# The third block of 512 columns of gates, pool output and conv output computed with the weights standing, two more small moves in the layer norm's step list

## The chip, the cores and the metric

One core of a Trainium2 chip runs the whole kernel. The metric is the device time of one launch in microseconds (us); lower is better. The kernel before is timed in three runs and profiled in one more. "Engine" means one of PE (TensorE, matmuls), DVE (VectorE), ACT (ScalarE), POOL (GpSimd) and SP (SyncE, which issues most loads).

## The reference, cut to what matters

One layer of a decoder trunk on 256 tokens plus 16 prepended meta tokens, model width 2048, everything in float32:

```python
u = rms_norm(h, g_pre_mix[l])
proj = u @ w_in[l]
z_pool, v_conv, g_conv, gate_a, gate_b = jnp.split(proj, splits, axis=-1)   # 1024,1024,1024,2048,2048
y_a = causal_multiscale_pool(z_pool, w_pool_grp[l], pool_scale[l]) @ w_pool_out[l]   # 1024 -> 2048
y_b = conformer_conv(v_conv, g_conv, ...) @ w_conv_out[l]   # 31 taps, layer norm, silu; 1024 -> 2048
m = jax.nn.sigmoid(gate_a) * y_a + jax.nn.sigmoid(gate_b) * y_b
h = h + rms_norm(m @ w_o[l], g_post_mix[l])
u = rms_norm(h, g_pre_mlp[l])
f = jnp.square(jax.nn.relu(u @ w_up[l])) @ w_down[l]
h = h + rms_norm(f, g_post_mlp[l])
```

The change lies between `proj` and `m`; everything from `m @ w_o` on stays as it is.

## The kernel before, in words

**Three-product arithmetic.** Every float32 operand is split into a high part and a low part. ACT makes the high part (`hi`, a cast), DVE the low part (`lo`, a subtraction that needs `hi`). A product is then hi·hi + hi·lo + lo·hi, so each weight chunk of 1 MB costs one load, one ACT cast (L287), one DVE subtraction (L290) and its matmuls. `fetch` (L348) opens the next chunk: it issues the load and the two splits for the chunk two ahead of the one that PE is about to use, and empties the list `late`.

**Columns in blocks of 512.** The two gates, the pool's output projection and the conv's output projection each have 2048 output columns, worked in four blocks `n` = 0..3. `TURNED` says how many of the four are done one way; the rest go the other way.

- Weights standing ("turned", `project`, n < TURNED): a 128x128 piece of the weights is the stationary operand and the activations stream past, `mm2`: one matmul of 512 columns (L556: high weights, both halves of the activations) and one of 256 (L562: low weights). The result has features on partitions, in four accumulators `j` of 128 features; each has two halves that ACT copies (L934) and DVE adds (L937). For a gate, DVE then scales by the token's norm factor (L952) and ACT takes the sigmoid of a 128x1024 tile (L953).
- Activations standing (`project_t`, n >= TURNED): a 128-token piece of the activations stands and the weights stream, three matmuls of 512 columns per k (L901). The result has tokens on partitions, in two accumulators `t`. ACT takes the sigmoid straight from the accumulator with the token's factor (L944).

For the mixed `m`, features must lie on partitions. Turned blocks come out that way. The others are transposed on PE (L1038, four 128x128 transposes per token half), then split from the transposed accumulator (L1042 on ACT, L1045 on DVE). Blocks 0 and 1 are also copied into `A` (L1071), from which four sums for a Strassen-like product with `w_o` are formed.

The order of the blocks is n = 0, 1, 2, 3 for each gate (`gate00` to `gate03`, then `gate10` to `gate13`), then eight small products of the pool's groups (`acc_grp`, evacuated to `y` by ACT at L978 and DVE at L979), then the pool output `po` in the order POOLS (blocks that are not turned first, then the turned ones), then the conv output `co` 0 to 3, then the products with `w_o`.

**What sets the order of the side work.** Each engine works its instructions off in the order in which they were written. DVE and ACT have work beside the splits: the pooling, the 31 conv taps (L621) and the layer norm over the conv's channels (`ln_...`). This work is a list, `pending`, of items with a cost. `drain` is called after each piece of a block and lets items be written whose cost fits the credit: a turned block gives 2.0 us per chunk in four portions, the other kind 2.9 us in two (pool output: 1.5 and 2.4). Two markers stand in the list. `LATER` ends the current portion. `FETCH` holds the list until `late` has been emptied by the next `fetch`. `late` holds work that is written a little later so that its engine does not stand waiting, such as the sigmoid of a gate that waits for PE, or the square root of the norm:

```python
def ln_root():
    ...
    def root():
        nc.scalar.activation(ln["q"], ln["var"], AF.Sqrt)
        warm_up(AF.Sigmoid)
    late.append(root)
```

The square root needs another table on ACT than the sigmoid, so `root` costs a table load, the square root, a second table load and a one-column sigmoid (`warm`).

The layer norm's items in their order are: sum over channels (`add4`, `add2`, then `low`, then markers, then `across`, two matmuls on PE with a matrix of ones, key "m"), mean, centre in two halves, sum of squares in the same way (key "v"), `ln_root`, `ln_newton` (five small DVE instructions, L506 to L510), and for each half of the channels `normed` (L871), eight ACT instructions (L876, L877), `swish` (L882), and the split of the result into `s_act` (L885 on ACT, L888 on DVE), which the conv output reads.

**Banks.** `acc_tile` hands out six accumulator banks in turn. An accumulator can be written again only when its last reader has finished. The pool output's first two accumulators are the banks of the first two group products.

The functions that the diff touches:

Of the kernel before, what the change touches and what calls it, by code (L numbers as in the profile page):

```python
# [15 lines left out]
P = 128  # L16
# [102 lines left out]
def hybrid_block(ctx: ExitStack, tc: tile.TileContext, ins: dict, out: bass.AP):  # L119
    nc = tc.nc  # L120
# [5 lines left out]
    NT = T // P  # L126
# [28 lines left out]
    def f32(ap):  # L155
        return ap.bitcast(F32)
# [4 lines left out]
    def misc_tile(name):  # L161
        return psB.tile([P, CW], F32, tag="misc", name=name)
# [5 lines left out]
    pending = []  # L168
    late = []
    LATER = (0, None)  # L170
    FETCH = (0, late)
# [43 lines left out]
    for h in range(PW // HALF_CW):  # L215
        stream += columns(w_in, 0, KD, h * HALF_CW, HALF)
    standing_chunks = set()
    TURNED = 2

    def with_standing(chunks, n):  # L220
        if n < TURNED:
            standing_chunks.update(range(len(stream), len(stream) + len(chunks)))
        return chunks
# [3 lines left out]
    stream.append((w_grp.rearrange("g (k p) c -> p (g k) c", p=P), (NG * GD // P, GD)))  # L227
    POOLS = [*range(TURNED, NB), *range(TURNED)]
    for w, nk, ns in ((w_pool_out, KP, POOLS), (w_conv_out, KC, range(NB))):
# [305 lines left out]
    def sum_rows(dst, parts):  # L535

        for n, part in enumerate(parts):
            nc.tensor.matmul(dst, ones, part, start=n == 0, stop=n == len(parts) - 1)
# [269 lines left out]
    def sum_items(key, dst, src):  # L808

        def add4():  # L810
            nc.vector.tensor_add(dst()[:, 0:4, :], src()[:, 0:4, :], src()[:, 4:8, :])

        def add2():
            nc.vector.tensor_add(dst()[:, 0:2, :], dst()[:, 0:2, :], dst()[:, 2:4, :])
            nc.vector.tensor_add(dst()[:, 0, :], dst()[:, 0, :], dst()[:, 1, :])
            parts[:] = [tmp.tile([P, T], F32R, tag="v", bufs=5, name=f"cs_{p}_{key}")
                        for p in ("hi", "lo")]
            late.append(lambda: nc.scalar.copy(parts[0], dst()[:, 0, :]))

        def low():  # L820
            nc.vector.tensor_sub(parts[1], dst()[:, 0, :], f32(parts[0]))

        def across():
            ln[key] = ps = misc_tile(f"cs_{key}")
            sum_rows(ps[:, :T], parts)
        parts = []
        return [(1.1, add4), (1.0, add2), FETCH, (0.4, low)] + [LATER] * 3 + [(0, across)]

    def ln_start():
        ln["sq"] = big.tile([P, KC, T], F32, tag="a", name="sq")  # L830
# [59 lines left out]
        return [(1.1, f) for f in (normed, swish, low, high)]  # L890

    ln_halves = ln_items(0), ln_items(QW)
    for half, step in ((0, 0), (1, 0), (0, 1), (1, 1)):
        pending += [FETCH, ln_halves[half][step]]

    def block_t(acc, hi, lo, act, kc, nk, t, ks=range(CK)):
        ts_ = slice(t * P, (t + 1) * P)
# [44 lines left out]
    def evac_gate(b, n):  # L942
        def f(t, acc):
            late.append(lambda: nc.scalar.activation(gate_t(b, n, t), acc, AF.Sigmoid,  # L944
                                                     scale=sc["r"][:, t:t + 1]))
        return f

    def evac_gate_turned(b, n):
        dst = turned(sg[b][:, n])

        def scaled():
            nc.vector.tensor_mul(dst, dst, rb[:, None, M:].broadcast_to([P, CK, T]))  # L952
            late.append(lambda: nc.scalar.activation(dst, dst, AF.Sigmoid))  # L953

        def f(j, acc):
            two_parts(dst[:, j, :], acc, scaled if j == CK - 1 else None)
        return f

    for b in range(2):
        sg[b] = big.tile([P, NB, NT * CW], F32, tag=f"s{b}", name=f"sg{b}")  # L960
        for n in range(NB):
            if n < TURNED:
                project(u, KD, evac_gate_turned(b, n), f"gate{b}{n}", shape=(CK, CW), fill=2.0, mid=True)
            else:
                project_t(u_of, KD, evac_gate(b, n), f"gate{b}{n}", fill=2.9, mid=n == TURNED)

# [44 lines left out]
    for n in POOLS:  # L1011
        if n < TURNED:
            project(y, KP, evac_pool_turned(n), f"po{n}", shape=(CK, CW), fill=1.5, mid=True)
# [9 lines left out]
    for keys, op in ((((0, 0), (0, 1)), {}), (((0, 1), (1, 1)), {"accum_op": ALU.add})):  # L1023
# [4 lines left out]
    m = big.tile([P, LINE + KD * 2 * T], F32R, tag="um", name="m")[:, LINE:].rearrange(  # L1028
        "p (k a t) -> p k a t", k=KD, a=2)
# [29 lines left out]
    def evac_conv_turned(n):  # L1059
        mt = turned(mts[:, n % 2 * NT:(n % 2 + 1) * NT, :].rearrange("p a c -> p (a c)"))  # L1060
        dst = m[:, n * CK:(n + 1) * CK]

        def merged():
            nc.vector.tensor_mul(mt, mt, turned(sg[1][:, n]))
            nc.vector.tensor_add(mt, mt, turned(sg[0][:, n]))
            late.append(lambda: nc.scalar.copy(dst[:, :, 0, :], mt))

        def low():
            nc.vector.tensor_sub(dst[:, :, 1, :], mt, f32(dst[:, :, 0, :]))
            for t in range(NT):  # L1070
                nc.scalar.copy(A[:, t, n], mt[:, :, t * P:(t + 1) * P])  # L1071

        def f(j, acc):
            two_parts(mt[:, j, :], acc, merged if j == CK - 1 else None)
            if j == CK - 1:
                blocks.append(low)
        return f

    assert TURNED == 2

    def s_act_of(k):
        return ln["out"][:, k, :, :]
# [2 lines left out]
    A = big.tile([P, NT, 2, CK, P], F32, tag="a", name="A")  # L1085
# [122 lines left out]
    for i, s in enumerate(steps):  # L1208
        key = raw_key(s)
# [5 lines left out]
        if s == "P6":  # L1215
            key = block_key("P", "3")
# [284 lines left out]
    high, low = u2_tiles(0, 1, CK, CK)  # L1501
# [56 lines left out]
    for k0 in (3 * CK, 3 * CK + 2):  # L1558
        high, low = u2_tiles(0, NT, k0, 2)
# [700 lines left out]
```

## Time and profile before

| what | us |
|---|---|
| median of 3 runs | 1177.66 (1177.63 to 1177.91) |
| profiled execution, its own time | 1178.29 |
| its span, first to last instruction | 1176.3 |
| PE busy | 1166.8 (99%) |
| DVE busy | 1030.1 (88%) |
| ACT busy | 704.2 (60%) |
| granted TensorE clock, mean | 0.998 |

The profiled execution took 0.63 us more than the median; 1.99 us of its time lie outside the span. Matmuls are pipelined, so a matmul's shown duration (390 ns for 512 columns) is longer than the distance to the next one; durations of PE are therefore read from start to start.

### The profile page before, as it was taken

The numbers are of one execution on the slowest core, as the hardware profiler recorded it, in microseconds if no ns is written. First come the engines' busy times: TensorE is split into PE (matmuls) and PEld (weight loads), VectorE is DVE, ScalarE is ACT, GpSimd is POOL, SyncE is SP. The second block draws the span as 40 slices with busy tenths as digits, with TensorE's granted clock in tenths as the row PEclk, the third lists the DMA queues.
The fourth block names the chain that finished last, engine by engine and source line by source line (L and its number), as shares of the span: only waits on it lengthen the run. The fifth ranks groups of instructions, "written<-read, shape, count | busy, mean of one in ns | idle before, by whom it ended". The sixth has DMA issues, their size and how long they took to land.

```text
span 1176.3 us, 16264 instructions
## 1 busy us (share of the span) xinstructions
PE 1166.8 (99%) x6503; PEld 1021.4 (87%) x6503; DVE 1030.1 (88%) x1145; ACT 704.2 (60%) x754; POOL 121.0 (10%) x103
## 2 busy tenths in 40 slices
PE   9999999999999999999999999999999999999997
PEld 9999998888888888898888888888888888888886
DVE  6899987988577899988998899988898978999888
ACT  6543345444486666766767566666666666676673
POOL 1133222222000001000000000000000001000000
PEclk9999999999999999999999999999999999999999
DMA  8789989999856957849899988988998898899884
GB/s 296 245 263 274 288 264 275 320 280 273 279 173 239 296 215 217 286 161 337 242 312 300 223 287 220 289 275 217 271 287 217 248 313 206 266 264 252 298 233 182
DMA packets 185419, 305.43 MB, mean 260 GB/s; under 512 B 5153, under 2 KB 93281, under 8 KB 182528
## 3 DMA queue, kind: packets, MB, share of 16 engines
q1 hardware_dynamic: 157440, 239.62, 59.2%
q0 software_dynamic: 27296, 64.12, 27.2%
q8 instruction: 51, 0.84, 0.3%
q10 hardware_dynamic: 608, 0.66, 0.2%
q14 instruction: 24, 0.20, 0.0%
HBM read 300.18 MB, written 29.36 MB: 280 GB/s over the span
## 4 chain that ended last, share of the span: by engine, by line
PE 99%; DVE 1%; DVEq 0%; issue 0%; ACT 0%; ACTq 0%
PE bank_u L556 19%; PE bank_a L1964 11%; PE bank_u L562 9%; PE acc_gate L901 7%; PE bank_b L1964 7%; PE acc_up L1964 7%; PE o_c L1311 6%; PE acc_gate L556 5%; PE acc_z L551 4%; PE acc_v L551 3%; PE acc_g L551 3%; PE acc_gate L562 2%; PE acc_vg L551 2%; PE acc_co L901 2%; PE acc_po L901 2%; PE acc_up L556 1%
## 5 line engine op out<-in xcount | busy, mean ns | idle before, releaser
L556 PE MATMUL bank_u<-m,hi 128*128 128x512 f32 x960 | 329.8, 390 | 0.0
L562 PE MATMUL bank_u<-m,lo 128*128 128x256 f32 x960 | 266.0, 277 | 0.1
L287 ACT CAST hi<-raw 128x2048 fp32r<-128x2048 f32 (+2 forms) x94 | 150.9, 1618 | 161.1 <-issue 35.0
L290 DVE TENSOR_TENSOR lo<-raw,hi 128x2048 fp32r<-128x2048 f32 (+2 forms) x94 | 180.1, 1926 | 45.6 <-ACT hi L287 45.4
L556 PEld LDWEIGHTS bank_u<-m,hi 128*128 128x128 f32 x960 | 180.3, 188 | 37.7
L1748 DVE TENSOR_TENSOR lo<-raw_m,hi 128x2048 fp32r<-128x2048 f32 x75 | 171.4, 2287 | 23.1 <-ACT hi L1744 22.9
L1744 ACT CAST hi<-raw_m 128x2048 fp32r<-128x2048 f32 x75 | 143.2, 1911 | 68.2 <-PE bank_u L556 32.5
L562 PEld LDWEIGHTS bank_u<-m,lo 128*128 128x128 f32 x960 | 180.4, 188 | 2.2 <-DVE lo L1748 0.5
L621 DVE SCALAR_TENSOR_TENSOR c<-a,taps,c 128x256 f32<-128x256 f32 x240 | 99.2, 483 | 0.1
L1748 DVE TENSOR_TENSOR lo<-raw_a,hi 128x2048 fp32r<-128x2048 f32 x30 | 68.6, 2287 | 10.4 <-ACT hi L1744 10.3
L1744 ACT CAST hi<-raw_a 128x2048 fp32r<-128x2048 f32 x30 | 57.3, 1911 | 28.4 <-PE bank_u L556 8.0
L1964 PE MATMUL bank_a<-hi,forms 128*128 128x512 f32 (+1 forms) x232 | 74.1, 383 | 0.0
L345 POOL COPY rows_of<-rows_of 128x1 f32<-128x1 f32 x24 | 48.8, 2033 | 227.6 <-ACT rows_of L344 227.6
L556 PE MATMUL acc_gate<-u_um,hi 128*128 128x512 f32 x208 | 71.5, 390 | 0.0
L1748 DVE TENSOR_TENSOR lo<-raw_c,hi 128x2048 fp32r<-128x2048 f32 x26 | 59.5, 2289 | 10.3 <-ACT hi L1744 10.3
L1825 ACT COPY half<-bank_u 128x256 f32<-128x256 f32 x60 | 22.2, 370 | 73.3 <-PE bank_u L562 73.3
L901 PE MATMUL acc_gate<-hi,u_um 128*128 128x512 f32 x208 | 65.8, 390 | 0.0
L1744 ACT CAST hi<-raw_c 128x2048 fp32r<-128x2048 f32 x26 | 49.6, 1907 | 23.0 <-PE bank_u L556 14.5
L1964 PE MATMUL acc_up<-hi,forms 128*128 128x512 f32 x184 | 60.6, 390 | 0.0
L1964 PE MATMUL bank_b<-hi,forms 128*128 128x512 f32 (+1 forms) x184 | 58.3, 381 | 0.0
L562 PE MATMUL acc_gate<-u_um,lo 128*128 128x256 f32 x208 | 57.5, 276 | 0.0
L1766 POOL DMA_DIRECT2D raw_m<-in_w_down_dram x17 | 21.6, 1270 | 323.9 <-DVE fourth_pair L1748 153.9
(458 smaller groups left out, 2590.6 us busy)
## 6 DMA issues: line engine op xcount, KB each, us to landing
raw<-in_w_in_dram SPq DMA_DIRECT2D x52, 1024.0 KB, 7.0
raw_m<-in_w_down_dram SPq DMA_DIRECT2D x37, 1024.0 KB, 8.2
raw_m<-in_w_up_dram SPq DMA_DIRECT2D x33, 1024.0 KB, 7.3
sum_P<-in_w_down_dram POOLq DMA_DIRECT2D x18, 1024.0 KB, 9.1
raw_m<-in_w_down_dram POOLq DMA_DIRECT2D x17, 1024.0 KB, 9.4
raw_c<-in_w_up_dram SPq DMA_DIRECT2D x14, 1024.0 KB, 7.1
raw_a<-in_w_down_dram SPq DMA_DIRECT2D x13, 1024.0 KB, 6.9
raw_a<-in_w_up_dram SPq DMA_DIRECT2D x11, 1024.0 KB, 6.6
```

What stands on the lines that cost most here:

```text
L287: nc.scalar.copy(hi[:, sl, cs], raw[:, sl, cs])
L290: nc.vector.tensor_sub(lo[:, sl, cs], raw[:, sl, cs], f32(hi[:, sl, cs]))
L345: nc.gpsimd.tensor_copy(marks[:, RH * M // 2 + a:RH * M // 2 + a + 1], marks[:, a:a + 1])
L551: nc.tensor.matmul(acc, w[:, k[0], cs], act[:, k[1], a, off:], start=first and n == 0, stop=last and n == 2)
L556: nc.tensor.matmul(acc.rearrange("p (a t) -> p a t", a=2)[:, :, ts], hi[:, k[0], cs], act[:, k[1], :, off + ts.start:off + ts.stop], start ...
L562: nc.tensor.matmul(acc[:, :T], lo[:, k[0], cs], act[:, k[1], 0, off:], start=False, stop=stop, skip_group_check=True)
L621: nc.vector.scalar_tensor_tensor(c, conv["a"][:, q, i:i + T], taps[:, q, i:i + 1], c, op0=ALU.mult, op1=ALU.add)
L901: nc.tensor.matmul(acc, act(kk)[:, a_, ts_], w_[:, k, :], start=kk == 0 and n == 0, stop=kk == nk - 1 and n == 2)
L1311: nc.tensor.matmul(acc, form(k, a_), box[w_][:, k, :], start=start and k == 0 and n == 0, stop=stop and k == CK - 1 and n == 2, skip_group ...
L1744: nc.scalar.copy(box["hi"], raw)
L1748: nc.vector.tensor_sub(box["lo"], raw, f32(box["hi"]))
L1964: nc.tensor.matmul(acc, forms[h][:, f, k, a_, :], box[w_][:, k, cs], start=start and k == 0 and n == 0, stop=stop and k == KH - 1 and n == ...
```

## The change

`TURNED` goes from 2 to 3, so block 2 of both gates, of the pool output and of the conv output changes from the second way to the first. POOLS becomes 3, 0, 1, 2. Of the copies into `A` blocks 0 and 1 alone are kept. One `LATER` more stands before `across` of the first sum. In the norm's last steps one `FETCH` is taken out, so that `normed` of the second half and `swish` of the first may be written in one stretch.

```diff
-    TURNED = 2
+    TURNED = 3
...
-        return [(1.1, add4), (1.0, add2), FETCH, (0.4, low)] + [LATER] * 3 + [(0, across)]
+        return [(1.1, add4), (1.0, add2), FETCH, (0.4, low)] + [LATER] * (4 if key == "m" else 3) + [(0, across)]
...
-    for half, step in ((0, 0), (1, 0), (0, 1), (1, 1)):
-        pending += [FETCH, ln_halves[half][step]]
+    pending += [FETCH, ln_halves[0][0], FETCH, ln_halves[1][0], ln_halves[0][1],
+                FETCH, ln_halves[1][1]]
...
         def low():
             nc.vector.tensor_sub(dst[:, :, 1, :], mt, f32(dst[:, :, 0, :]))
-            for t in range(NT):
-                nc.scalar.copy(A[:, t, n], mt[:, :, t * P:(t + 1) * P])
+            if n < 2:
+                for t in range(NT):
+                    nc.scalar.copy(A[:, t, n], mt[:, :, t * P:(t + 1) * P])
...
-    assert TURNED == 2
+    assert TURNED == 3
```

Three places show how the instructions move. The numbers behind the names are buffer numbers; they differ between the two kernels and carry no meaning.

First, ACT at the end of the gates. `hi` is the high part of a chunk, `ln_q` the norm's square root, `sg1` the second gate, `acc_gate13_0` and `_1` the two accumulators of the last gate block, `y` the evacuated group products. Before:

```order
L287 CAST hi_57_3224<-raw_57_3223 128x2048
L855 ACT_TABLE_LOAD
L855 ACTIVATE ln_q_3221<-ln_var_3219 128x256
L375 ACT_TABLE_LOAD
L375 ACTIVATE warm_107<-ones_105 128x1
L944 ACTIVATE sg1_2583<-acc_gate13_0_3111,r_in_530 128x512
L944 ACTIVATE sg1_2583<-acc_gate13_1_3112,r_in_530 128x512
L287 CAST hi_58_3259<-raw_58_3258 128x2048
L978 ACTIVATE y_3255<-acc_grp_0_3264,vecs_110 128x256
```

ACT at the same place in the changed kernel:

```order
L287 CAST hi_57_3301<-raw_57_3300 128x2048
L944 ACTIVATE sg1_2616<-acc_gate13_0_3192,r_in_530 128x512
L944 ACTIVATE sg1_2616<-acc_gate13_1_3193,r_in_530 128x512
L855 ACT_TABLE_LOAD
L855 ACTIVATE ln_q_3335<-ln_var_3333 128x256
L375 ACT_TABLE_LOAD
L375 ACTIVATE warm_107<-ones_105 128x1
L287 CAST hi_58_3343<-raw_58_3342 128x2048
L978 ACTIVATE y_3337<-acc_grp_0_3348,vecs_110 128x256
```

The two table loads and the square root moved from ahead of the last gate's sigmoids to behind them. On PE the two matmuls of `across` for "v" moved with them, from inside the last gate block to behind its last matmul.

Second, DVE at the pool output, where the norm's last steps stand. `lo` is the low part of a chunk, `c` the conv's channels, `s_act` the norm's split result, `pairs` the room for a turned block's halves. Before:

```order
L290 TENSOR_TENSOR lo_61_3420<-raw_61_3418,hi_61_3419 128x2048
L882 TENSOR_TENSOR c_622<-c_622,sq_2934 128x1024 x2
L290 TENSOR_TENSOR lo_62_3461<-raw_62_3459,hi_62_3460 128x2048
L995 TENSOR_TENSOR sg0_1895<-acc_po3_0_3416,sg0_1895 128x512
L888 TENSOR_TENSOR s_act_3458<-c_622,s_act_3458 128x4x256
L995 TENSOR_TENSOR sg0_1895<-acc_po3_1_3417,sg0_1895 128x512
L888 TENSOR_TENSOR s_act_3458<-c_622,s_act_3458 128x4x256
L290 TENSOR_TENSOR lo_63_3501<-raw_63_3499,hi_63_3500 128x2048
L290 TENSOR_TENSOR lo_64_3539<-raw_64_3537,hi_64_3538 128x2048
L937 TENSOR_TENSOR pairs_3341<-pairs_3341,acc_po0_0_3495 128x256
```

DVE at the same place in the changed kernel:

```order
L882 TENSOR_TENSOR c_622<-c_622,sq_3054 128x1024
L290 TENSOR_TENSOR lo_61_3507<-raw_61_3505,hi_61_3506 128x2048
L882 TENSOR_TENSOR c_622<-c_622,sq_3054 128x1024
L290 TENSOR_TENSOR lo_62_3555<-raw_62_3553,hi_62_3554 128x2048
L937 TENSOR_TENSOR pairs_3425<-pairs_3425,acc_po0_0_3501 128x256
L1005 TENSOR_TENSOR sg0_1895<-pairs_3425,sg0_1895 128x256
L937 TENSOR_TENSOR pairs_3425<-pairs_3425,acc_po0_1_3502 128x256
```

Only one block that is not turned (block 3) now stands ahead of block 0, so block 0's first addition follows the split of chunk 62 where it followed that of chunk 64. The norm's last split (L888) moved behind block 0's additions.

Third, DVE from the conv output's third block to the products with `w_o`. `mts` holds the mixed block, `m` its split form, L1064 and L1065 multiply by the gate and add the pool's share. Before:

```order
L1054 TENSOR_TENSOR mts_3683<-acc_co2_0_3868,sg1_2583 128x512
L1055 TENSOR_TENSOR mts_3683<-mts_3683,sg0_1895 128x512
L1054 TENSOR_TENSOR mts_3683<-acc_co2_1_3869,sg1_2583 128x512
L1055 TENSOR_TENSOR mts_3683<-mts_3683,sg0_1895 128x512
L290 TENSOR_TENSOR lo_73_3950<-raw_73_3948,hi_73_3949 128x2048
L1045 TENSOR_TENSOR m_3681<-mt_2_0_3978,m_3681 128x4x128
L1045 TENSOR_TENSOR m_3681<-mt_2_1_3985,m_3681 128x4x128
L290 TENSOR_TENSOR lo_74_3994<-raw_74_3992,hi_74_3993 128x2048
L1054 TENSOR_TENSOR mts_3683<-acc_co3_0_3946,sg1_2583 128x512
```

DVE at the same place in the changed kernel:

```order
L937 TENSOR_TENSOR mts_3795<-mts_3795,acc_co2_0_3980 128x256
L937 TENSOR_TENSOR mts_3795<-mts_3795,acc_co2_1_3981 128x256
L937 TENSOR_TENSOR mts_3795<-mts_3795,acc_co2_2_3982 128x256
L937 TENSOR_TENSOR mts_3795<-mts_3795,acc_co2_3_3983 128x256
L1064 TENSOR_TENSOR mts_3795<-mts_3795,sg1_2616 128x1024
L1065 TENSOR_TENSOR mts_3795<-mts_3795,sg0_1895 128x1024
L290 TENSOR_TENSOR lo_73_4082<-raw_73_4080,hi_73_4081 128x2048
L1069 TENSOR_TENSOR m_3793<-mts_3795,m_3793 128x4x256
L290 TENSOR_TENSOR lo_74_4118<-raw_74_4116,hi_74_4117 128x2048
L1054 TENSOR_TENSOR mts_3795<-acc_co3_0_4078,sg1_2616 128x512
```

The block's own work on DVE is written as seven instructions where it was six, and the eight transposes on PE that stood between them are gone. From the products with `w_o` on, every engine's instructions stand in the same order in both kernels.

## The prediction

> **What bounds the kernel now.** I read the page's busy shares and the chain that ended last, then the starts of PE's stages in the timeline, then ACT and DVE around the places where the order changes.
>
> ```profile
> PE 1166.8 (99%) x6503; PEld 1021.4 (87%) x6503; DVE 1030.1 (88%) x1145; ACT 704.2 (60%) x754; POOL 121.0 (10%) x103
> PE 99%; DVE 1%; DVEq 0%; issue 0%; ACT 0%; ACTq 0%
> 153.10:421.60 268.50, 268.50 (x1407) 230.95 (x1406) 219.46 (x263) 142.84 (x157) 37.81 (x32) 1.00 0.85 262
> ```
>
> The chain is PE for 99%. The third row (columns: window, length, then busy time of PE, weight loads, DVE, ACT, POOL, then clock) covers all that the diff touches: PE never pauses, DVE has 49.0 us free, ACT 125.7. So only two things move the time: PE's own work, and any wait that a new order puts in front of PE. The starts of the stages give PE's work (columns: start, shown duration, engine, line):
>
> ```profile
> 153.13 0.40 PE L556 MATMUL acc_gate<-u_um,hi 128*128 128x512 f32 x1
> 196.66 0.40 PE L901 MATMUL acc_gate<-hi,u_um 128*128 128x512 f32 x1
> 240.20 0.40 PE L556 MATMUL acc_gate<-u_um,hi 128*128 128x512 f32 x1
> 333.56 0.40 PE L901 MATMUL acc_po<-hi,y 128*128 128x512 f32 x1
> 355.35 0.40 PE L556 MATMUL acc_po<-y,hi 128*128 128x512 f32 x1
> 377.12 0.39 PE L556 MATMUL acc_co<-s_act,hi 128*128 128x512 f32 x1
> 398.88 0.40 PE L901 MATMUL acc_co<-hi,s_act 128*128 128x512 f32 x1
> 421.59 0.39 PE L1311 MATMUL o_c<-hi,m 128*128 128x512 f32 x1
> 415.24 1.03 PE L1038 MATMUL mt<-ident,mts 128*128 128x128 f32 x8
> ```
>
> **Term 1, the blocks themselves: 0.** Two turned gate blocks take 196.66 - 153.13 = 43.53 us, two of the other kind 240.20 - 196.66 = 43.54. Pool output: 21.79 against 21.77. Both kinds stream as many columns. The page "TensorE: Matmul & The Clock Gate" of the Trainium skill (section "Wait — 56ns, not 53.3ns?") speaks against the change here: beside its columns each warm matmul costs some 2.5 ns, and the change makes 192 matmuls of 256 columns out of 96 of 512; an estimate by that rule is 96 x 2.5 ns = 0.24 us more. The two gate pairs, which differ by 64 matmuls, come out 0.01 us apart, so the trace does not agree, and I take 0.
>
> **Term 2, the transposes: -0.95.** Two turned conv blocks take 398.88 - 377.12 = 21.76 us, the two others 421.59 - 398.88 = 22.71. The excess is the eight transposes of block 2 (1.03 us with the last one's tail); block 3's are made later, inside the products with w_o, and stay. The change removes the eight.
>
> **Term 3, a new wait ahead of the pool output: +2.65.** Here ACT's order matters. Before:
>
> ```profile
> 322.35 1.91 ACT L287 CAST hi<-raw 128x2048 fp32r<-128x2048 f32 x1 [3.53 <-PE acc_gate L901]
> 324.28 1.28 ACT L855 ACT_TABLE_LOAD   x1
> 325.57 0.42 ACT L855 ACTIVATE ln_q<-ln_var 128x256 f32<-128x256 f32 x1
> 325.99 1.28 ACT L375 ACT_TABLE_LOAD   x1
> 327.29 0.20 ACT L375 ACTIVATE warm<-ones 128x1 f32<-128x1 f32 x1
> 327.40 1.30 ACT L944 ACTIVATE sg<-acc_gate,r_in 128x512 f32<-128x512 f32 x2
> 328.60 1.90 ACT L287 CAST hi<-raw 128x2048 fp32r<-128x2048 f32 x1
> 330.39 2.41 ACT L978 ACTIVATE y<-acc_grp,vecs 128x256 fp32r<-128x256 f32 x6
> ```
>
> The square root with its two table loads (324.28 to 327.40, 3.1 us) lies where ACT would otherwise wait for PE to finish the last gate block. DVE and PE behind it:
>
> ```profile
> 327.59 0.39 PE L901 MATMUL acc_gate<-hi,u_ux 128*128 128x512 f32 x1
> 322.11 0.28 PE L538 MATMUL cs_v<-cs_hi_v,ones 128*128 128x256 f32 x1
> 322.54 0.42 DVE L851 TENSOR_SCALAR ln_var<-cs_v 128x256 f32<-128x256 f32 x1 [1.40 <-PE cs_v L538]
> 330.53 2.29 DVE L290 TENSOR_TENSOR lo<-raw,hi 128x2048 fp32r<-128x2048 f32 x1 [3.94 <-ACT hi L287]
> 332.74 3.22 DVE L979 SCALAR_TENSOR_TENSOR y<-acc_grp,vecs,y 128x256 fp32r<-128x256 f32 x8
> ...
> L979 DVE SCALAR_TENSOR_TENSOR y<-acc_grp,vecs,y x8: 476/476/479, 332.7 to 335.5; 128x256 fp32r<-128x256 f32 x8
> ```
>
> The eight at 332.74 take 0.476 us each (last row: least, median and greatest, in ns) at a pitch of 0.39, so the first low part of y is ready at 333.22, and PE takes it up at 333.56, without a wait but with only 0.34 us to spare. PE's first matmul of the pool output needs exactly that instruction, because it also frees the first bank.
>
> In the changed kernel the norm's list runs one portion later: `across` for "v" comes behind the last gate matmul, and `root` behind both sigmoids. Step by step: the last gate matmul starts 0.23 earlier (the two matmuls of `across`, 0.11 apart, now follow it), at 327.36, and its shown end is 327.75. The second sigmoid, 0.65, runs to 328.43. The table load ends at 329.73 (ln_var, 0.4 us behind `across`, is there by 328.4), the square root at 330.15, the second load at 331.44, and the cast of chunk 58 starts 0.11 behind the warm instruction's start, at 331.56 instead of 328.60. Everything behind it on ACT and DVE moves by these 2.96 us: y's first low part ends at 333.22 + 2.96 = 336.18. PE arrives at 333.56 and waits 2.6 to 2.7 us, I take 2.65. Once it runs, it uses one y per 0.68 us and DVE makes one per 0.39, so no further wait follows there. Queued behind the late cast are the y parts (who wait on ACT) and `ln_newton`, normed and the split of chunk 59 on DVE; the last has some 2.5 us of cover. Bounds: not below 1.4 (if one table load of 1.28 overlapped something), not above 3.2 (if the sigmoid's start slipped by its own 0.65).
>
> **Term 4, a wait for a bank in the second turned pool block: +0.35.** From the rows before:
>
> ```profile
> 341.44 1.22 DVE L871 TENSOR_TENSOR c<-c,ln_r 128x1024 f32<-128x1024 f32 x1
> 342.70 0.60 ACT L876 ACTIVATE sq<-c,vecs 128x256 f32<-128x256 f32 x1 [1.54 <-DVE c L871]
> 347.22 1.89 ACT L287 CAST hi<-raw 128x2048 fp32r<-128x2048 f32 x1
> 353.54 1.89 ACT L287 CAST hi<-raw 128x2048 fp32r<-128x2048 f32 x1
> 355.46 2.29 DVE L290 TENSOR_TENSOR lo<-raw,hi 128x2048 fp32r<-128x2048 f32 x1 [0.57 <-ACT hi L287]
> 357.67 0.68 DVE L995 TENSOR_TENSOR sg<-acc_po,sg 128x512 f32<-128x512 f32 x1
> 365.54 0.41 DVE L937 TENSOR_TENSOR pairs<-pairs,acc_po 128x256 f32<-128x256 f32 x1
> ```
>
> The norm's eight ACT instructions per half take 347.22 - 342.70 = 4.52. After term 3 `normed` of the first half starts 2.9 us later (344.36), the eight end at 350.1, a cast (1.8), the second eight, and the cast of chunk 62 run from 356.4 to 358.3; its low part on DVE ends its slot at 360.6 (355.46 to 357.67: 2.21). Only then comes block 0's first addition, to 361.0. That addition frees the bank which PE wants for block 1's third accumulator, at 336.2 + 2 x 10.89 + 2.72 = 360.7. A wait of 0.35; bounds 0 and 0.8, since it is the end of a long chain. Before, additions like it (365.54) had cover because the norm was through.
>
> **What I cost at nothing.** DVE gets some 9 us more: per gate four additions of 0.41 and one scaling of 1.2, twice; in the pool output 2.0; in the conv output 1.3. They fall into its 49.0 free us. ACT's twelve extra copies and one larger sigmoid per gate fall into 125.7. The smaller portions write 9 us less of the pending list (0.9 x 4 chunks x 2 gates, 0.9 x 2 in the pool), so the norm's last split lands in block 1 of the pool output, about 10 us ahead of the conv output that reads it. The extra LATER makes PE reach `across` of "m" 6.8 us into its stretch; the operand needs a cast (1.9), a split (2.3) and its own 0.4 first, 4.7 in all, so 2.1 us are spare (0.8 without it). SP's loads keep number and order; POOL's are untouched. The one place without much cover is the start of the products with w_o:
>
> ```profile
> 398.90:422.00 23.10, 23.10 (x108) 19.21 (x107) 20.53 (x20) 11.30 (x11) 0.00 (x0) 1.00 0.67 214
> 432.14 0.68 DVE L1303 TENSOR_TENSOR forms_o<-A,forms_o 128x512 fp32r<-128x512 f32 x1
> 433.84 0.39 PE L1311 MATMUL o_c<-hi,forms_o 128*128 128x512 f32 x1
> ```
>
> DVE's form is ready at 432.82, PE wants it at 433.84: 1.0 to spare. DVE comes there later against PE by at most 1.3 (more work) + 0.95 (PE's transposes gone), less the 2.57 us that it idled in the stage. I take 0, bound 1.2.
>
> **Sum.** 0 - 0.95 + 2.65 + 0.35 = +2.05 us. On the profiled execution that is 1178.29 + 2.05 = 1180.34; the median before stands 0.63 lower, so the forecast for the median is 1177.66 + 2.05 = 1179.7, that is +0.17%. I count less than 0.2% (2.4 us: below 1175.3, above 1180.0) as no change that a measurement can tell.
>
> **Rivals.**
> - The wait of term 3 is hidden: something lets ACT run the loads early, or PE arrives late anyway. Then only the transposes count: 1177.66 - 0.95 = 1176.7. The instruction order speaks against it. Chance 0.12.
> - The pause slows the clock. At launch PE's matmuls of 128 columns come twice as slowly as later, though the granted clock is written as 1.00:
>
> ```profile
> 1.13 3.35 PE L452 MATMUL idle<-rb 128*128 128x128 f32 x14 [1.13 <-DVE rb L366]
> 5.96 1.28 PE L452 MATMUL idle<-rb 128*128 128x128 f32 x6
> ```
>
> 0.21 us each until about 6.9, against 0.11 for the transposes at 415.24: 5.8 us at half pace. If a pause of 2.65 us brings that back for as long, it costs half of 5.8, 2.9 us, and the time is 1182.6, slower. It decides once 0.3 us are lost so. No pause of that length is in the trace to judge by. The Trainium skill, same page, section "Part 1: The HAM clock gate (the "warmup" mystery)", puts the fall to half clock behind an idle window of about 3.4 us; by that rule a pause of 2.65 is too short. Chance 0.08.
> - DVE is late at the products with w_o, or term 3 or 4 at its upper bound: 0.3 to 1.2 more, 1180.1 to 1181. Chance 0.22, slower too.
>
> **How the numbers follow.** The forecast's own case, terms 3 and 4 near their values, 0.58: 1178.9 to 1180.0, no change. With the first rival, no change has 0.12 + 0.55, slower 0.08 + 0.22 + 0.01, and faster keeps 0.02, since nothing on PE's path could give 2.4 us. The range goes from the first rival's 1176.7 to 1181.0, leaving out the clock and some of either tail.
>
> **What would show it.** Right: on PE a gap of about 2.6 us ahead of the first L901 of `acc_po`, released by DVE's y (L979); ACT with the table loads behind the sigmoids; the three turned conv blocks at 32.6 us and no transposes at block 2; a small gap in the second turned pool block, released by L937. Wrong: PE without a gap there; 128-column pace doubled behind it; new gaps on L1311 behind forms_o or on gates behind L290.

## The result, and the profile after

| | us |
|---|---|
| before, median of 8 runs beside it | 1177.91 (1177.39 to 1178.36) |
| after, median of 8 runs | 1181.66 (1180.43 to 1184.25) |
| ratio of after to before | 1.0034, 95% interval 1.0024 to 1.0043 |
| profiled execution of after, its own time | 1182.13 (before 1178.29) |
| its span | 1180.3 (before 1176.3) |

The change costs 3.75 us by the medians and 3.84 us by the two profiled executions. The forecast was +2.05 us, with a range up to 1181.0: the result lies above it.

The page of after, its busy times, then the starts of PE's stages in the timeline (start, shown duration, engine, line):

```profile
PE 1167.9 (99%) x6591; PEld 1024.7 (87%) x6591; DVE 1037.3 (88%) x1162; ACT 708.6 (60%) x767; POOL 117.6 (10%) x103
153.30:425.60 272.30, 269.69 (x1494) 234.75 (x1493) 226.68 (x280) 147.02 (x170) 34.36 (x32) 1.00 0.85 259
153.32 0.39 PE L556 MATMUL acc_gate<-u_um,hi 128*128 128x512 f32 x1
333.69 0.28 PE L551 MATMUL acc_grp<-d,lo 128*128 128x256 f32 x1
336.51 0.50 PE L901 MATMUL acc_po<-hi,y 128*128 128x512 f32 x1 [2.54 <-DVE y L979]
381.08 0.39 PE L556 MATMUL acc_co<-s_act,hi 128*128 128x512 f32 x1
414.68 0.40 PE L901 MATMUL acc_co<-hi,s_act 128*128 128x512 f32 x1
425.62 0.39 PE L1312 MATMUL o_c<-hi,m 128*128 128x512 f32 x1
```

The busy shares say 99% for PE as before; only the window row shows that PE now pauses (269.69 busy of 272.30). By stage, from the starts here and those of before:

| stage | before | after | difference |
|---|---|---|---|
| start of the gates (nothing ahead of it was touched) | 153.13 | 153.32 | +0.19 |
| gates, up to the first group product (328.06 after, 327.81 before) | 174.68 | 174.74 | +0.06 |
| group products, up to the pool output | 5.75 | 8.45 | +2.70 |
| pool output | 43.56 | 44.57 | +1.01 |
| conv output | 44.47 | 44.54 | +0.07 |
| from the products with w_o to the end | 754.74 | 754.72 | -0.02 |

The 2.70 is one gap. ACT and DVE there in after, with the bracket's idle time and its releaser:

```profile
328.02 0.69 ACT L944 ACTIVATE sg<-acc_gate,r_in 128x512 f32<-128x512 f32 x1 [2.03 <-PE acc_gate L901]
328.73 1.28 ACT L855 ACT_TABLE_LOAD   x1
330.44 1.28 ACT L375 ACT_TABLE_LOAD   x1
331.85 1.89 ACT L287 CAST hi<-raw 128x2048 fp32r<-128x2048 f32 x1
335.98 3.22 DVE L979 SCALAR_TENSOR_TENSOR y<-acc_grp,vecs,y 128x256 fp32r<-128x256 f32 x8
```

ACT waits 2.03 us for the second sigmoid's accumulator and only then loads its tables, the cast comes at 331.85 instead of 328.60, DVE's y at 335.98 instead of 332.74, and PE takes y up at 336.51.

The pool output's 1.01 and the conv's 0.07 need the pace of single matmuls. PE and DVE around the second turned pool block, then PE near the end of the turned conv blocks:

```profile
360.12 0.39 PE L556 MATMUL acc_po<-y,hi 128*128 128x512 f32 x1
360.34 0.28 PE L562 MATMUL acc_po<-y,lo 128*128 128x256 f32 x1
360.46 0.39 PE L556 MATMUL acc_po<-y,hi 128*128 128x512 f32 x1
361.02 0.28 PE L562 MATMUL acc_po<-y,lo 128*128 128x256 f32 x1
361.37 0.50 PE L556 MATMUL acc_po<-y,hi 128*128 128x512 f32 x1
358.70 2.29 DVE L290 TENSOR_TENSOR lo<-raw,hi 128x2048 fp32r<-128x2048 f32 x1 [0.57 <-ACT hi L287]
360.90 0.41 DVE L937 TENSOR_TENSOR pairs<-pairs,acc_po 128x256 f32<-128x256 f32 x1
...
412.58 0.39 PE L556 MATMUL acc_co<-s_act,hi 128*128 128x512 f32 x1
412.93 0.40 PE L556 MATMUL acc_co<-s_act,hi 128*128 128x512 f32 x1
413.28 0.39 PE L556 MATMUL acc_co<-s_act,hi 128*128 128x512 f32 x1
```

Two things are to be seen. At 361.02 the next matmul comes 0.35 us later instead of 0.11: the wait of 0.24 for the bank that DVE's addition at 360.90 frees. The first matmul behind it takes 0.34 to the next start instead of 0.23 (361.37 to 361.71), as the one at 336.51 does (to 336.84). And behind that wait a pair of one 512- and one 256-column matmul takes 0.35 us (412.58, 412.93, 413.28), where ahead of it it took 0.34 (360.12 to 360.46). From 361.37 to 414.68, where the block of the other kind begins, lie 152 such pairs: (53.31 - 0.11 for the first matmul after the wait) / 152 = 350 ns a pair, against 340, so 152 x 0.010 = 1.5 us. The granted clock is 1.00 throughout. So the pool output's 1.01 is 0.11 (first matmul after the gap) + 0.24 + 0.11 (bank wait and the matmul after it) + 56 pairs x 0.010; the conv's 0.07 is 96 pairs x 0.010 = 0.96 less 0.89 for the transposes that are gone.

### The profile page after: what moved, and what is told of

It is laid out like the page before. It is cut to its first block, busy times and chain, and to the rows that moved or that the text cites. A ratio compares the mean times of both kernels' runs of the same rounds, so it can differ in the third digit from the quotient of the medians.

```text
span 1180.3 us, 16472 instructions
## 1 busy us (share of the span) xinstructions
PE 1167.9 (99%) x6591; PEld 1024.7 (87%) x6591; DVE 1037.3 (88%) x1162; ACT 708.6 (60%) x767; POOL 117.6 (10%) x103
## 4 chain that ended last, share of the span: by engine, by line
PE 96%; DVE 2%; ACT 1%; issue 0%; DVEq 0%; ACTq 0%
PE bank_u L556 18%; PE bank_a L1965 11%; PE bank_u L562 9%; PE acc_gate L556 7%; PE bank_b L1965 7%; PE acc_up L1965 7%; PE o_c L1312 6%; PE acc_z L551 4%; PE acc_gate L562 4%; PE acc_gate L901 4%; PE acc_v L551 3%; PE acc_g L551 3%; PE acc_vg L551 2%; PE acc_co L556 2%; PE acc_up L556 1%; PE acc_po L556 1%
## 5 line engine op out<-in xcount | busy, mean ns | idle before, releaser
L562 PE MATMUL bank_u<-m,lo 128*128 128x256 f32 x960 | 265.4, 276 | 0.3 <-DVE lo L1749 0.3
L562 PEld LDWEIGHTS bank_u<-m,lo 128*128 128x128 f32 x960 | 180.2, 188 | 2.4 <-DVE lo L1749 0.7
L556 PE MATMUL acc_gate<-u_um,hi 128*128 128x512 f32 x312 | 107.3, 389 | 0.0
L562 PE MATMUL acc_gate<-u_um,lo 128*128 128x256 f32 x312 | 86.1, 276 | 0.0
L556 PEld LDWEIGHTS acc_gate<-u_um,hi 128*128 128x128 f32 x312 | 58.6, 188 | 12.2
L345 POOL COPY rows_of<-rows_of 128x1 f32<-128x1 f32 x24 | 45.2, 1883 | 233.2 <-ACT rows_of L344 233.2
L562 PEld LDWEIGHTS acc_gate<-u_um,lo 128*128 128x128 f32 x312 | 58.6, 188 | 0.0
```

Source lines behind the costliest of these rows:

```text
L345: nc.gpsimd.tensor_copy(marks[:, RH * M // 2 + a:RH * M // 2 + a + 1], marks[:, a:a + 1])
L556: nc.tensor.matmul(acc.rearrange("p (a t) -> p a t", a=2)[:, :, ts], hi[:, k[0], cs], act[:, k[1], :, off + ts.start:off + ts.stop], start ...
L562: nc.tensor.matmul(acc[:, :T], lo[:, k[0], cs], act[:, k[1], 0, off:], start=False, stop=stop, skip_group_check=True)
```

## The experiments

Theory after the result: three separate losses, the extra `LATER` (ACT's table loads behind the last sigmoids, 2.7 us), the bank wait (0.35), and a slow pace of the turned blocks, 1.5 us, which something sets. Rivals: the third block itself costs the 2.7 us; the slow pace belongs to the third block, not to the wait. Medians below stand beside runs of before on the same chip, whose medians are 1177.59 (experiments 1 to 4), 1177.81 (5 and 7 to 9) and 1177.70 (6 and 11). What is read from a profile holds for the one execution that was profiled.

**1. The square root ahead of the sigmoids again**, by another way than the old order:

```diff
-    [LATER] * (4 if key == "m" else 3)
+    [LATER] * (4 if key == "m" else 2)
...
-        late.append(root)
+        late.insert(0, root)
```

> The changed kernel with the norm's square root and its two table loads written ahead of the last gate's two sigmoids (one LATER less before across of v, root put first in the list). Theory W (waits): the 2.8 us gap of PE ahead of the pool output comes from the table loads behind the sigmoids, so it is gone. Block 0's first addition then ends at about 358.1, where PE wants its bank at 358.1: no wait or under 0.1. If PE does not wait there, matmuls go 227/113 ns apart to the end of the conv output and the time is 1177.0 (before 1177.9 - 0.95 + 0.1); if the least wait is enough for the slow pace (232/117 ns), it is about 1178.5. Rival P (pace of position): three turned blocks after each other run at the slow pace by themselves; then 1178.5 with no wait at all.

Measured: 1179.61 (11 runs, 1177.53 to 1180.85), ratio 1.0015 (1.0006 to 1.0024). The expectation missed: the gap ahead of the pool output did not go but shrank from 2.70 to 1.03 us, and a bank wait of 0.24 and the slow pace (152 pairs) stayed. ACT in this kernel:

```profile
323.75 1.28 ACT L855 ACT_TABLE_LOAD   x1
326.43 0.42 ACT L855 ACTIVATE ln_q<-ln_var 128x256 f32<-128x256 f32 x1 [1.39 <-DVE ln_var L851]
326.85 1.28 ACT L375 ACT_TABLE_LOAD   x1
328.25 1.25 ACT L944 ACTIVATE sg<-acc_gate,r_in 128x512 f32<-128x512 f32 x2
```

The first load is covered, but the square root waits 1.39 us for DVE's `ln_var`. So the gap follows the place of the loads, and this way of moving them covers only part of it.

**2. Spare banks for the second turned pool block**, so that its last two accumulators wait for nobody:

```diff
-        accs = [acc[:, :width] for acc in acc_tiles(name, cw // P)]
+        tiles = acc_tiles(name, cw // P if name != "po1" else 2)
+        tiles += [misc_tile(f"acc_{name}_{j}") for j in range(len(tiles), cw // P)]
+        accs = [acc[:, :width] for acc in tiles]
```

> The changed kernel with two of the four accumulators of pool block 1 in the two spare banks, so that none has to wait for block 0's additions; ACT's order stays. Theory W: the 2.8 us gap stays, the 0.35 us wait at 361 is gone, and with it the slow pace behind it (53 us at +2.8%, 1.5 us): 1181.7 - 0.35 - 1.5 = 1179.9. Rival P: the wait is gone but matmuls still go 232/117 ns apart from there on: 1181.3.

Measured: 1181.59 (7 runs, 1180.06 to 1183.64), ratio 1.0028 (1.0017 to 1.0040). In the trace it went as the theory had it: no bank wait and no slow pace behind it, the turned blocks of pool and conv output at 32.65 and 32.64 us where after has 33.56 and 33.60, and the gap stayed. But the median is that of after, 1181.66, and not the 1179.9 expected, since something else stood in the profiled execution, which was the slowest of the seven (columns of the windows as above, clock before the DMA share):

```profile
336.05 0.79 PE L903 MATMUL acc_po<-hi,y 128*128 128x512 f32 x1 [2.54 <-DVE y L981]
330.00:336.00 6.00, 3.51 (x30) 3.31 (x28) 2.69 (x3) 5.99 (x11) 0.00 (x0) 0.95 0.14 55
336.00:342.00 6.00, 5.95 (x14) 4.69 (x15) 5.86 (x12) 2.00 (x2) 0.00 (x0) 0.50 0.52 178
342.00:348.00 6.00, 6.00 (x27) 4.90 (x27) 4.75 (x4) 3.21 (x4) 0.00 (x0) 0.98 0.39 130
```

Behind the same pause as in after, the granted clock was 0.50 for 6.83 us, and in 6.00 us PE ran 14 matmuls instead of some 27. Block 3 of the pool output took 13.89 us (336.05 to 349.95) where after needs 11.02, so 2.9 us were lost. After's own profile has the same pause and 1.00. So such a pause slows the clock in some executions and not in others. Each execution also lists its mean clock: here the two fastest, 1180.06 and 1180.18, have 0.998, the others, 1181.00 to 1183.64, have 0.996 and 0.997.

**3. The edits of experiments 1 and 2 together.**

> Both of these edits. Theory W: neither gap nor wait, pace 227/113 ns throughout but for the 4 us behind across of m in gate block 2: 1177.9 - 0.95 + 0.1 = 1177.0, 0.9 faster than before. Rival P: slow pace in the pool and conv blocks all the same: 1178.5.

Measured: 1178.26 (11 runs, 1177.45 to 1179.07), ratio 1.0005 (0.9997 to 1.0014). Against experiment 1 this is -1.35 us, for the bank wait and the slow pace (by the traces 0.35 + 1.5, less a new wait of 0.21 at the transposes of block 3, which is 1.6).

**4. The third block alone**: the extra `LATER` and the new chunks of the norm's last steps undone.

```diff
-    [LATER] * (4 if key == "m" else 3)
+    [LATER] * 3
...
-    pending += [FETCH, ln_halves[0][0], FETCH, ln_halves[1][0], ln_halves[0][1],
-                FETCH, ln_halves[1][1]]
+    for half, step in ((0, 0), (1, 0), (0, 1), (1, 1)):
+        pending += [FETCH, ln_halves[half][step]]
```

> The changed kernel with the other two parts undone: four chunks for the norm's last steps and three LATER before across of m, so that only the third turned block is left of the change. Theory W: ACT's order at the end of the gates is the same, gap and wait as well: 1181.7, within 0.4. Rival M (the small moves cost the time): 1178 or less.

Measured: 1179.38 (11 runs, 1177.84 to 1180.24), ratio 1.0012 (1.0004 to 1.0021). The expectation missed. There is no gap ahead of the pool output, but the bank wait is 1.2 us, with the slow pace behind it (152 pairs). ACT, PE and DVE in this kernel:

```profile
324.29 1.28 ACT L855 ACT_TABLE_LOAD   x1
327.41 1.31 ACT L944 ACTIVATE sg<-acc_gate,r_in 128x512 f32<-128x512 f32 x2
357.99 0.28 PE L562 MATMUL acc_po<-y,lo 128*128 128x256 f32 x1
359.30 0.50 PE L556 MATMUL acc_po<-y,hi 128*128 128x512 f32 x1 [1.03 <-DVE pairs L937]
357.69 1.22 DVE L882 TENSOR_TENSOR c<-c,sq 128x1024 f32<-128x1024 f32 x1
358.83 0.41 DVE L937 TENSOR_TENSOR pairs<-pairs,acc_po 128x256 f32<-128x256 f32 x1
```

The loads stand ahead of the sigmoids, as before the change. And the four chunks put `swish` (L882) straight ahead of the addition that PE waits for.

**5. The third block and the three chunks, without the extra `LATER`.**

```diff
-    [LATER] * (4 if key == "m" else 3)
+    [LATER] * 3
```

> The changed kernel without the extra LATER; three turned blocks and three chunks stay. Theory L (the LATER moved the norm's list one portion on and so the square root behind the sigmoids): no gap ahead of the pool output; a wait for block 0's addition of 0.1 to 1.2 us and the slow pace behind it stay: 1179.4. Rival C (the three chunks are what moved it): gap of 2.7 us, 1181.7.

Measured: 1178.40 (11 runs, 1177.11 to 1179.63), ratio 1.0006 (0.9997 to 1.0015). No gap; the bank wait is down to 0.05 us (PE L562 at 357.54, next at 357.70 instead of 357.65), and still the slow pace begins there (152 pairs). Each against its own runs of before, after stands at +3.75, this kernel at +0.59 and that of experiment 4 at +1.79. So the extra step of patience costs 3.2 us, and the three chunks are worth 1.2.

**6. The two small parts alone**, with two turned blocks as before (against the kernel before):

```diff
-    [LATER] * 3
+    [LATER] * (4 if key == "m" else 3)
...
-    for half, step in ((0, 0), (1, 0), (0, 1), (1, 1)):
-        pending += [FETCH, ln_halves[half][step]]
+    pending += [FETCH, ln_halves[0][0], FETCH, ln_halves[1][0], ln_halves[0][1],
+                FETCH, ln_halves[1][1]]
```

> The two small parts alone, with two turned blocks as before: the norm's last steps in three chunks, and one more step of patience for its first sum. By the written order the square root's two table loads then stay ahead of the last gate's sigmoids. Theory (the pause needs the third block and the step of patience together): no pause, no bank wait, no slow pace, time as before, 1177.6 to 1178.0. Rival (the step of patience costs by itself, wherever the loads stand): 1 to 3 us more.

Measured: 1177.72 (11 runs, 1177.02 to 1178.72), ratio 1.0000 (0.9991 to 1.0009). No gap, no bank wait, no slow pace at the pool output. The step of patience costs nothing by itself: with two turned blocks the loads stay ahead of the sigmoids (at 323.48 and 325.19, the sigmoids at 326.60). Only the third block and the step together push them behind.

**7 and 8. What sets the slow pace?** Kernel before, with matmuls of a matrix of ones put in between the pairs at one place of four blocks, in two arrangements (`extra` writes so many matmuls of so many columns into a spare bank; its results are used by nobody):

```diff
+            if n == 0:
+                after.extend([nop] * 5 + [extra(u, M, ("1x512", "2x256")[b])])
...
+        if n < 2:
+            after.extend([nop, extra(y, 0, ("2x256", "3x512")[n])])
```

> The kernel before (two turned blocks), with a few matmuls with a matrix of ones put into turned blocks, their results unused: one of 512 columns in gate00, two of 256 in gate10, two of 256 in pool block 0, three of 512 in pool block 1. No wait is added. Theory I (interruption: any break in the alternation of a 512- and a 256-column matmul, by a wait or by other matmuls, sets the slow pace of 232/117 ns, which lasts until a block of the other kind begins): slow from each of the first three places to the end of its turned stretch (40, 40 and 37 us at 2.8%, together 3.2 us; the extra matmuls themselves 1.6): 1182.4. Whether three of 512 end the slow pace in pool block 1 is open. Rival S (only a wait for a semaphore sets it): 227/113 ns everywhere, 1179.2.

The other arrangement:

```diff
+                after.extend([nop] * 5 + [extra(u, M, ("1x256", "3x512")[b])])
...
+            after.extend([nop, extra(y, 0, ("1x256", "1x512")[n])])
```

> The same with other matmuls: one of 256 columns in gate00, three of 512 in gate10, one of 256 in pool block 0 and one of 512 in pool block 1. Theory I: slow pace from each place that breaks the alternation, up to 3.2 us, so up to 1182.2. Rival S: fast everywhere, 1179.0. If parity decides (two 256 in a row or two 512 in a row), the places differ: gate00 and pool block 0 (256 behind 256) slow, gate10 not.

Measured: 1180.13 (10 runs), ratio 1.0020 (1.0011 to 1.0029), and 1180.11 (10 runs), ratio 1.0019 (1.0009 to 1.0028). In each, one place alone set the slow pace, the one with three matmuls of 512 columns. The first kernel there, and where it ended:

```profile
369.01 0.39 PE L556 MATMUL acc_po<-y,hi 128*128 128x512 f32 x1
369.35 0.85 PE L966 MATMUL spare_3x<-y,ones 128*128 128x512 f32 x3
370.04 0.40 PE L556 MATMUL acc_po<-y,hi 128*128 128x512 f32 x1
370.39 0.40 PE L556 MATMUL acc_po<-y,hi 128*128 128x512 f32 x1
...
400.84 0.40 PE L901 MATMUL acc_co<-hi,s_act 128*128 128x512 f32 x1
```

Ahead a pair takes 0.34 (369.01 to 369.35), behind it 0.35, for 88 pairs, up to the first block of the other kind. In the second kernel it was 104 pairs from 249.3 to 285.7, again up to a block of the other kind. The times fit: 4 x 0.227 + 4 x 0.114 + 88 x 0.010 = 2.2 us for the first, 2.3 measured. So no wait is needed to set the slow pace; one matmul of 512 columns, or one or two of 256, did not set it at these places. Neither "any break of the rhythm" nor "only a wait" holds.

Two short matmuls can set it, though. In every kernel here with three turned blocks the two matmuls of `across` for "m" (L538, 256 columns each) stand inside gate block 2, with no wait that the profile shows. In after:

```profile
301.60 0.28 PE L538 MATMUL cs_m<-cs_hi_m,ones 128*128 128x256 f32 x1
301.84 0.39 PE L556 MATMUL acc_gate<-u_um,hi 128*128 128x512 f32 x1
302.19 0.39 PE L556 MATMUL acc_gate<-u_ux,hi 128*128 128x512 f32 x1
```

Behind them a pair takes 0.35 (301.84 to 302.19), for 12 or 16 pairs, up to the last gate block. That is 0.1 to 0.2 us of the gates.

**9. The third block alone, with spare banks and the transposes of block 3 one step later**: the edits of experiments 4 and 2, and

```diff
-        if i == 0:
+        if i == 1:
             for t in range(NT):
                 m_last(t)
```

> Three turned blocks alone (both small parts undone), with the spare banks in pool block 1 and the last block's transposes one product later (behind X02). Theory W with L: no gap, no bank wait, fast pace but for 5 us in gate block 2: 1177.7 - 0.95 + 0.15 = 1176.9. Rival: the slow pace or a new wait takes the gain: 1177.7 or more.

Measured: 1182.68 (5 runs), ratio 1.0039 (1.0026 to 1.0052), the slowest of all. Up to the products with w_o it went as meant: 419.79 - 152.11 = 267.68 us against 268.46 before, so -0.78. Then:

```profile
427.95 1.03 PE L1040 MATMUL mt<-ident,mts 128*128 128x128 f32 x8
432.73 0.80 PE L1314 MATMUL o_a<-hi,m 128*128 128x512 f32 x1 [3.75 <-DVE m L1047]
431.00:437.80 6.80, 5.07 (x12) 4.01 (x13) 5.07 (x6) 0.20 (x1) 0.56 (x1) 0.50 0.82 281
```

The later transposes make `m` late by 3.75 us, and that pause too is followed by half clock. Of the five executions one lists a mean clock of 0.999 and took 1179.87 us; the other four list 0.995 to 0.997 and took 1182.62 to 1183.71.

**10. How long a pause takes the clock down**: a kernel of its own, which computes nothing of the layer. Bursts of 60 to 75 matmuls, ten lengths of pause between them (PE waits for a chain of DVE instructions), each eight times, in one execution. A pause is the distance between the starts of the two matmuls less the 0.23 us that one takes; the idle time in a row's bracket is 0.16 shorter, since the shown duration is longer than 0.23.

```python
for r in range(8):
    for g in [1, 2, 4, 5, 6, 7, 8, 9, 10, 12]:
        for i in range(n):
            nc.tensor.matmul(acc, ..., start=i == 0, stop=i == n - 1)
        for i in range(g):
            nc.vector.tensor_mul(sink[:, :256], acc[:, :256], x_in[:, 1, :256])
```

> A kernel of its own: 80 bursts of 60 to 75 matmuls of 512 columns, and between them pauses of PE of about 0.7 to 4.4 us (a chain of 1 to 12 DVE multiplications that read the accumulator), ten lengths, eight times each. Nothing of the layer is computed; the output is x with a small sum added. Theory H (a pause can halve the clock, the more often the longer it is): none after pauses of 1 us, some after 2.7 us, all from some 3.4 to 6.8 us on; each fall lasts whole multiples of 3.41 us (6.83 in the run with the spare banks). Rival T (a fixed threshold): none below one length, all above.

| pause, us | 0.68 | 1.14 | 2.05 | 2.51 | 2.97 | 3.43 | 3.89 | 4.35 | 4.80 | 5.72 |
|---|---|---|---|---|---|---|---|---|---|---|
| followed by half clock | 0 of 8 | 0 of 8 | 3 of 8 | 4 of 8 | 6 of 8 | 7 of 8 | 8 of 8 | 8 of 8 | 8 of 8 | 7 of 7 |

No single length divides them: from 2.05 to 3.43 us both outcomes occur. Two pauses of the same length, 2.05 us. Of each the matmuls behind it, then a window there with its clock (in the first, 8 of the 18 matmuls of 5.98 us came 0.43 us apart instead of 0.23):

```profile
269.74 5.98 PE L41 MATMUL acc<-hi,act 128*128 128x512 f32 x18 [1.90 <-DVE sink L44]
469.36 1.43 PE L41 MATMUL acc<-hi,act 128*128 128x512 f32 x5 [1.89 <-DVE sink L44]
270.00:274.00 4.00, 4.00 (x12) 3.09 (x12) 0.00 (x0) 0.00 (x0) 0.00 (x0) 0.57 0.00 0
466.50:474.00 7.50, 5.61 (x25) 4.32 (x24) 1.70 (x4) 0.00 (x0) 0.00 (x0) 1.00 0.00 0
```

Each fall lasted 3.41 or 6.83 us, once or twice 3.41. A pause of after's length, 2.7, lies between the columns with 4 and 6 of 8.

**11. The best that the parts give**: the third block and the three chunks, without the extra `LATER`, with the spare banks (the edits of experiments 5 and 2).

> The third turned block and the three chunks, without the extra step of patience, and with the last two accumulators of the second turned pool block in banks that nothing else holds there. Theory (the extra step makes the 2.7 us pause and the half clock behind it; the bank wait sets the slow pace of 1.5 us; the transposes gone are worth 0.95): no pause ahead of the pool output, no bank wait, fast pace up to the conv output, a wait of 0.2 to 0.8 us at the transposes of m ahead of the products with w_o, because PE arrives there sooner; 1177.8 - 0.95 + 0.12 + 0.5 = 1177.5, against 1178.4 without the spare banks. Rival (the slow pace comes from the third block itself, not from the wait): the slow pace stays, 1178.4 as before.

Measured: 1177.15 (11 runs, 1176.27 to 1178.59), ratio 0.9997 (0.9989 to 1.0006). It beats the changed kernel, and cannot be told from before. Up to the products with w_o it is 267.68 us, 0.78 faster than before. PE and DVE behind that:

```profile
422.89 0.66 PE L1040 MATMUL mt<-ident,mts 128*128 128x128 f32 x4
424.22 0.66 PE L1040 MATMUL mt<-ident,mts 128*128 128x128 f32 x4 [0.67 <-DVE mts L1057]
419.22 2.28 DVE L290 TENSOR_TENSOR lo<-raw,hi 128x2048 fp32r<-128x2048 f32 x1
423.47 0.69 DVE L1057 TENSOR_TENSOR mts<-mts,sg 128x512 f32<-128x512 f32 x1
```

PE arrives at the transposes of block 3 before DVE has their operand: 0.18 us ahead of the first four, 0.84 ahead of the others (against back to back). These 1.02 us take back all that the third turned block had gained. Each against its own runs of before, it stands 1.14 us below experiment 5 (-0.55 against +0.59): the bank wait and the slow pace are gone, and part of that is lost again here, where experiment 5 waited 0.30.

## Why the prediction was wrong

Point by point, by its own steps:

- **Term 1, blocks' pace 0: right as far as it went.** Gates +0.06. But it took for granted that a turned block has one pace. It has two, 340 and 350 ns a pair. The slow one is not a price per matmul, since the pool and conv output of experiment 11 run three turned blocks at the fast one. The page "TensorE: Matmul & The Clock Gate" of the Trainium skill (section "Wait — 56ns, not 53.3ns?") gives each warm matmul some 2.5 ns beside its columns; the two gate pairs of before, 43.53 and 43.54 us with 64 matmuls between them, set that rule aside, and rightly.
- **Term 2, transposes -0.95: right**, -0.89 by the stages of after, and -0.92 in experiment 11 (419.99 - 376.44 = 43.55 against 44.47).
- **Term 3, +2.65: right in size and mechanism**, 2.70 and 0.11 for the first matmul. The instruction order had shown it. It is the step of patience on top of the third block that makes it (experiments 4 to 6).
- **Term 4, +0.35: right in place and cause**, behind the addition named (L937 behind the low part of a chunk). The wait itself is 0.24, within the bounds; that the first matmul behind it adds 0.11, which the term did not hold, and brings the sum to 0.35 is luck. At the same bank experiments 4 and 5 wait 1.2 and 0.05.
- **What was costed at nothing: this step failed.** Behind term 4 the prediction let PE run on at one pace, so that a wait costs its own length and no more. The bank wait set the slow pace for 152 pairs, 1.5 us in the profiled execution. With spare banks wait and slow pace are gone from the traces (experiments 2, 3 and 11), and the medians stand lower by 1.35 (3 against 1) and 1.14 (11 against 5, each against its own runs of before). The sum of the stages up to the products with w_o, +4.03, is the forecast's 2.05 + 1.5 + 0.11 for the first matmul behind the gap, 0.06 in the gates, 0.06 less for the transposes, 0.05 for term 3 and 0.19 at the start. The price stood in the trace of before, outside the stages that the prediction read. In the products with w_up, 48 pairs from 530.80 to 547.71, where a block of 512-column matmuls alone begins, take 350 ns each:

```profile
530.80 0.40 PE L556 MATMUL bank_u<-m,hi 128*128 128x512 f32 x1
531.15 0.40 PE L556 MATMUL bank_u<-m,hi 128*128 128x512 f32 x1
531.50 0.39 PE L556 MATMUL bank_u<-m,hi 128*128 128x512 f32 x1
```

- **The products with w_o, 0, bound 1.2: right for after**, where PE came late. Where PE comes in time, DVE is late: 1.02 (experiment 11). DVE's extra work came to 7.2 us (226.68 against 219.46 in the windows), not 9, which changed nothing.
- **The rival of the clock: real, and given too little (0.08).** Half clock follows such pauses in experiments 2, 9 and 10, and in experiment 2 it cost the 2.9 us that the rival had named. The page "TensorE: Matmul & The Clock Gate" of the Trainium skill (section "Part 1: The HAM clock gate (the "warmup" mystery)") asks for an idle window of about 3.4 us; the runs do not agree, since pauses of 2.05 us brought it in 3 of 8. What the 3.41 us fit is the length of the falls. The profiled execution of after had no fall, and its 3.84 us are accounted for without one. That settles this execution and not the median. A fall of 3.41 us lowers the mean clock of an execution by 3.41 x 0.5 / 1180 = 0.0014. Seven of after's eight executions list 0.997, against 19 of the 77 of before that stand beside the experiments. So falls in some of after's executions are likely, but 0.997 comes without a pause too, and after's spread of 3.8 us does not show them, since experiments 4 and 5, without such a pause, spread over 2.4 and 2.5. Experiment 2, without bank wait and slow pace, has the median of after. How much of the median's 3.75 us is slow pace and how much is clock stays open.

**What stays open.** What a break must have to set the slow pace is not settled. At the pool's bank waits of 0.05, 0.24 and 1.2 us all set it, and so did three extra matmuls of 512 columns and the two of 256 of `across`; one extra matmul of 512 or two of 256 did not. In each case between the gates and the conv output it lasted to the next block in which the activations stand. The order of the matmuls alone does not decide: in the products with w_up, where all kernels have the same order, the 48 pairs are slow in the profiled executions of before and of six experiments, and fast in those of after and of four others. Nor does a wait always set it: farther on there, behind 564.14 in before, a wait of 0.27 us is followed by 340 ns a pair. Whether 0.05 us of wait can be taken away without the spare banks wasn't tried.

## What to carry to other kernels

An engine at 99% busy can still lose microseconds that no wait shows: compare the start-to-start pace of the same pair of instructions ahead of a wait and behind it, not only the length of the wait. When work on the bounding engine is removed, look at the next place where another engine delivers to it; in experiment 11 0.9 us of transposes saved came back as 1.0 us of waiting a few microseconds later. A step moved behind an instruction that waits for PE (here two table loads behind the last sigmoids) can cost nearly its whole length on the far side, here 2.7 of 3.1 us, so a longer wait in a list is to be tried together with the change of credit that it meets.

## What the runs showed of the hardware that was not expected

- Alternating matmuls of 512 and 256 columns go at 340 or at 350 ns a pair at a granted clock of 1.00. The slow pace, once set, held for 12 to 152 pairs, until a block of 512-column matmuls alone began. The same 48 pairs in the same order went at the one pace in some executions and at the other in others.
- In experiment 10 half clock came after pauses of 2.05 us in 3 of 8, of 2.97 in 6 of 8, and of 3.89 and more in all 31; it came after none of the 16 of 1.14 and less. It lasted 3.41 or 6.83 us. It began 2.5 to 5.7 us after the start of the last matmul ahead of the pause (2.2 in experiment 2), so it can fall on matmuls behind the pause.
